# Expert weights in longer rows, into pairs of neighbouring buffers

## The chip, the cores and the metric

One core of a Trainium2 chip runs the whole program. The time is the device time of one execution in microseconds (us). Three executions of the kernel before are the measure it is held against.

## What is computed

Two transformer blocks run one after the other on 512 tokens of width 1024, batch 1, all in float32. The first has an attention with three branches and a linear recurrence (RG-LRU); the second has a chunked mLSTM, a differential attention and, at its end, a mixture of 32 experts, which is what the change is about:

```python
def hierarchical_moe(h, w_rg, b_rg, w_re, b_re, w_gate, w_up, w_down):
    hf = h.reshape(-1, d_)
    ...
    y = jnp.zeros_like(hf)
    for e in range(N_EXPERTS):                      # 32 experts, two of them per token
        act = jax.nn.silu(hf @ w_gate[e]) * (hf @ w_up[e])     # 1024 -> 256 each
        y = y + combine[:, e:e + 1] * (act @ w_down[e])        # 256 -> 1024
    return y.reshape(b_, s_, d_)
...
x = x + gate2 * hierarchical_moe(h2, ...)
```

Gate and up weights of one expert are 1024 x 512 floats (2 MB), its down weights 256 x 1024 (1 MB), so that the experts together are 100.7 MB of weights, each read once.

## The kernel before, in words

**Recording and planning.** The code doesn't issue instructions as it runs. Class `Plan` records every operation as a node with what it reads and writes (`record`, line 216), and `order` then places the nodes one after the other: at each step it takes, over the five engines, the node that can start first by its own prices, and gives its output tiles a buffer. `issue` (line 400) emits them all in that order; line 409 is therefore the line of every instruction in the profile, and groups go by tile names. Two nodes share a buffer by names like `t4.7`: a tile with that tag waits for all users of the tile before it.

**Buffers.** `SIZES` gives the tags: `t4` has 38 buffers of 128 x 1024 floats (4 KB in each of 128 partitions), `a2` 15 and `p2` 9 buffers of 128 x 512. Nearly everything large lives in `t4`: a loaded weight slab (`gt`, `gr`, `wp`), its two parts `h` and `l` in float32r (`slab`: high part by a cast, low part by a subtraction, so that three matmuls give float32 accuracy), the transposed hidden state `hTh`/`hTl` (`new_hT`), rows of `x`, and the expert tiles `wg`. Loads named in `FREE` (`wg`, `wd`) may be issued up to 9000 nodes early, as soon as a buffer is free.

**The experts** (`experts`, line 1804). The router places the tokens of two experts, i and i+16, in 128 rows, 64 each; there are 16 such rounds. A round gathers its rows from `x2d` in HBM (`fetch`: an indirect DMA of POOL into one of two tiles X), transposes them on PE into XT, multiplies them by the two experts' gate/up weights into H, activates, transposes (`aT`), multiplies by the down weights into two banks, scales into Y, and adds Y's rows to the output by an indirect DMA of POOL. In H the two experts use the two halves of PE's columns at once. Weights come by SP, and by SP alone:

```python
for q in range(4):                       # wg: 128 x 2 x 512, 4 KB rows, 512 KB a load
    for e in range(2):
        nc.sync.dma_start(ws[e], I["wgu"][i + 16 * e, q])
...
for k in range(2):                       # wd: 128 x 512, 2 KB rows, 256 KB a load
    for h in range(2):
        for e in range(2):
            nc.sync.dma_start(w, I["wd"][i + 16 * e, k][:, h * 512:(h + 1) * 512])
```

So a round has eight `wg` loads and eight `wd` loads. Completion of SP's loads is counted by eight semaphores in turn (DMAHW0 to DMAHW7); a load waits until the load eight before it has landed. `experts` runs once straight through; a loop behind it repeats it if an expert has more than 64 tokens, which doesn't occur here.

**What lies ahead of the first round.** `route_chunk` writes four pieces of normalised rows to `x2d` and the residual to the output, by SP's queue; `route`, `slots` and `weights` compute the row numbers `si` and the factors `wt` on DVE and PE. The first gather needs the four `x2d` writes and `si`.

Of the kernel before, what the change touches and what calls it, by code (L numbers as in the profile page):

```python
# [134 lines left out]
class Tile:  # L135
    def __init__(self, plan, tag, shape, dt, name, keep, given=None):
        self.plan, self.tag, self.name, self.dt, self.shape, self.keep = plan, tag, name, dt, list(shape), keep
        self.got = given
# [31 lines left out]

class Node:
# [7 lines left out]
class Plan:  # L179
# [20 lines left out]
    def tile(self, tag, shape, dt, name, keep=False):  # L200
        return Tile(self, tag, shape, dt, name, keep).view()
# [62 lines left out]
    def order(self):  # L264
# [9 lines left out]
        for nd in nodes:  # L274
            for t in nd.tiles:
# [5 lines left out]
                prof[t.tag][start:end] += 1  # L281
# [3 lines left out]
        for nd in nodes:  # L285
            for t in nd.births:
                rest[t.tag] += not nd.load
# [13 lines left out]
        while len(out) < N:  # L301
# [3 lines left out]
            for e, lst in ready.items():  # L305
# [4 lines left out]
                for nd in lst:  # L310
# [7 lines left out]
                    if nd.births:  # L318
                        ok = nd.load or nd.i - p < 400
                        need = {}  # L320
                        for t in nd.births:
# [3 lines left out]
                            k = need[t.tag] = need.get(t.tag, 0) + 1  # L325
# [7 lines left out]
                            s = max(s, tg.free[k - 1][0])  # L333
# [17 lines left out]
            for t in nd.births:  # L351
# [6 lines left out]
                t.slot = tg.free.pop(0)[1]  # L358
                rest[t.tag] -= not nd.load
                if p < t.first:  # L360
                    prof[t.tag][p:t.first] += 1
# [16 lines left out]
            for t in nd.tiles:  # L378
                t.left -= 1
                if t.left == 0 and not t.keep and self.tags[t.tag].space != "dram":  # L380
                    r = max(k.done[1] + (200.0 if k.done[2] == "PE" or t.space == "psum" else 130.0)
                            for k in [nd] + [k for _, k in t.writes + t.reads])
                    insort(self.tags[t.tag].free, (r, t.slot))
                    if p <= t.last:
                        prof[t.tag][p:t.last + 1] -= 1
# [122 lines left out]
class Net:  # L508
    def __init__(self, tc, ctx, I, out, upto="all", dbg=None):
# [5 lines left out]
        self.kept, self.stand = [], {}  # L515
# [9 lines left out]
    SIZES = {"t4": 38, "a2": 15, "p2": 9, "vm": 4, "sq128": 3, "c1k": 4}  # L525

    def start(self):

        self.nc = Plan(self.tc, self.scratch, self.stand)
        self.nc.tag("dram", "dram", [], self.make)  # L530
# [7 lines left out]
    def make(self, t):  # L538
        if t.space == "dram":
            return self.pools["dram"].tile(t.shape, t.dt, name=t.name)  # L540
        return self.pools[t.space].tile(t.shape, t.dt, name=t.name, tag=f"{t.tag}.{t.slot}", bufs=1)

    def tile(self, tag, shape, dt, name, keep=False, bufs=None, space="sbuf"):
        if tag not in self.nc.tags:
            self.bufs.setdefault(tag, bufs or self.SIZES[tag])
            kept = {t.slot for t in self.kept if t.tag == tag}
            self.nc.tag(tag, space, [k for k in range(self.bufs[tag]) if k not in kept], self.make)
        v = self.nc.tile(tag, shape, dt, name, keep)
# [4 lines left out]
    def t4(self, name, shape=(128, 1024), dt=F32, keep=False):  # L553
        return self.tile("t4", list(shape), dt, name, keep)

# [21 lines left out]
    def pair4(self, name):  # L577

        t = [self.t4(f"{name}{i}", (128, 2, 512), F32R) for i in range(2)]
        return [t[k // 2][:, k % 2, :] for k in range(4)]  # L580
# [1434 lines left out]
```

## Time and profile before

| | us |
|---|---|
| median of three executions | 1121.15 (1118.64 to 1123.18) |
| the profiled execution | 1121.38 |
| its span, first to last instruction | 1119.5 |
| PE busy | 1043.2 (93%) |
| DVE busy | 636.0 (57%) |
| ACT busy | 394.1 (35%) |
| POOL busy | 187.8 (17%) |
| HBM read | 212.91 MB, 206 GB/s over the span |

A span is the time in which instructions run; 1.9 us of the execution's time lie around it. Busy shares are means over the whole span, and stages differ: a table by stage tells more than the page. In a stage, the engine or queue that is never idle sets the pace; what others wait for there is the thing to look up. DMA share is the mean busy share of the core's 16 DMA engines, from the times of their packets, and can come out a little over 1.

### The profile page before, as it was taken

The page shows a single profiled execution, that of the slowest core. Times are in us where ns is not written, and L with a number is a line of the kernel's source. Part 1 is how long each engine was busy: PE and PEld are TensorE (multiplying, and loading weights), DVE is VectorE, ACT ScalarE, POOL GpSimd, SP SyncE. Part 2 cuts the span into 40 slices and gives each one's busy share as a digit, 9 for nine tenths or more (in the row PEclk, how much of TensorE's full clock was granted, in tenths as well). Part 3 has the DMA queues.
Part 4 walks back from the last instruction along what each step waited for, and adds up shares of the span by engine and source line. Part 5 has one row for each costly group of instructions (what it writes and reads, how often), then busy time and mean ns, then how long its engine had stood idle before and what let it go on. Part 6 is the DMA issues. An engine that isn't in the chain of part 4 may idle for free. (4 is left out here: it accounts for less than half of the span.)

```text
span 1119.5 us, 14485 instructions
## 1 busy us (share of the span) xinstructions
PE 1043.2 (93%) x5194; PEld 724.3 (65%) x5194; DVE 636.0 (57%) x1433; ACT 394.1 (35%) x803; POOL 187.8 (17%) x173
## 2 busy tenths in 40 slices
PE   9999999999999999999999999999996999877875
PEld 7776666777887777786687887788785333322221
DVE  4757788695654746976978876535714223222221
ACT  6235566562222326436653333222412112111110
POOL 1201134001011224401311001100201122210101
PEclk9998998999999999999999999999996999999997
DMA  9981100234444807160232423546699999999995
GB/s 350 339 323 43 39 1 20 76 99 132 122 139 162 274 38 280 53 263 11 94 147 85 164 95 113 169 131 225 227 359 366 323 368 343 365 376 346 387 368 166
DMA packets 77374, 223.43 MB, mean 200 GB/s; under 512 B 12164, under 2 KB 13772, under 8 KB 77296
## 3 DMA queue, kind: packets, MB, share of 16 engines
q1 hardware_dynamic: 72544, 213.94, 53.0%
q0 software_dynamic: 4608, 8.40, 3.1%
q8 instruction: 43, 0.70, 0.3%
q14 instruction: 35, 0.29, 0.1%
q10 hardware_dynamic: 144, 0.10, 0.0%
HBM read 212.91 MB, written 17.32 MB: 206 GB/s over the span
## 5 line engine op out<-in xcount | busy, mean ns | idle before, releaser
L409 PE MATMUL H<-wg,XT 128*64 128x512 f32 x512 | 128.8, 606 | 11.0 <-DMA wg<-in_wgu 8.0
L409 PE MATMUL b<-hTh,gth 128*128 128x512 f32 x464 | 122.9, 402 | 0.0
L409 PE MATMUL b<-hTl,gth 128*128 128x512 f32 x464 | 121.4, 398 | 0.0
L409 PE MATMUL b<-hTh,gtl 128*128 128x512 f32 x464 | 119.7, 397 | 0.0
L409 POOL TENSOR_TENSOR gtl<-gt,gth 128x1024 fp32r<-128x1024 f32 x23 | 57.5, 2501 | 262.6 <-ACT gth L409 243.5
L409 PEld LDWEIGHTS b<-hTh,gth 128*128 128x128 f32 x464 | 86.2, 189 | 23.7 <-issue 4.2
L409 PEld LDWEIGHTS b<-hTh,gtl 128*128 128x128 f32 x464 | 86.6, 188 | 20.4 <-issue 0.5
L409 PEld LDWEIGHTS b<-hTl,gth 128*128 128x128 f32 x464 | 86.2, 188 | 20.1 <-issue 0.9
L409 PEld LDWEIGHTS H<-wg,XT 128*64 128x64 f32 x512 | 37.7, 137 | 86.5 <-issue 52.4
L409 DVE TENSOR_SCALAR XT<-b,mod,mod 128x128 f32<-128x128 f32 x64 | 24.2, 408 | 78.4 <-PE H L409 69.0
L409 PE MATMUL b<-wd,aT 128*64 128x512 f32 x256 | 60.7, 612 | 7.7 <-ACT aT L409 5.0
L409 DVE SCALAR_TENSOR_TENSOR ada_acc<-ada_w,cols,ada_acc 128x1024 f32<-128x1024 f32 x42 | 60.2, 1434 | 8.5 <-DMA ada_w<-in_w_ada 8.5
L409 DVE SCALAR_TENSOR_TENSOR Y<-b,wt,gate 128x512 f32<-128x512 f32 x32 | 24.0, 751 | 68.1 <-PE b L409 65.0
L409 ACT ACTIVATE XT<-b,mod,mod 128x128 f32<-128x128 f32 x64 | 27.4, 459 | 88.5 <-PE H L409 71.1
L409 ACT ACTIVATE gth<-gt 128x1024 fp32r<-128x1024 f32 x53 | 55.4, 1050 | 6.7 <-DMA gt<-in_wb 6.7
L409 PE MATMUL b<-grh,hTh 128*128 128x512 f32 x192 | 56.1, 404 | 0.0
L409 PE MATMUL b<-grl,hTh 128*128 128x512 f32 x192 | 55.6, 399 | 0.0
L409 PE MATMUL b<-grh,hTl 128*128 128x512 f32 x192 | 55.0, 398 | 0.0
L409 POOL DMA_INDIRECT out_rows<-Y,si x16 | 25.3, 1583 | 159.3 <-DVE Y L409 144.0
L409 ACT ACTIVATE grh<-gr 128x1024 fp32r<-128x1024 f32 (+2 forms) x39 | 39.7, 1032 | 29.8 <-DMA gr<-in_wo 8.7
L409 DVE TENSOR_TENSOR gtl<-gt,gth 128x1024 fp32r<-128x1024 f32 x35 | 42.6, 1223 | 10.8 <-ACT gth L409 8.9
L409 DVE SCALAR_TENSOR_TENSOR mg<-mg,b 128x512 f32<-128x512 f32 x32 | 21.9, 686 | 43.4 <-PE b L409 43.4
(374 smaller groups left out, 1830.6 us busy)
## 6 DMA issues: line engine op xcount, KB each, us to landing
wg<-in_wgu SPq DMA_DIRECT2D x128, 512.0 KB
wd<-in_wd SPq DMA_DIRECT2D x128, 256.0 KB
gt<-in_wb SPq DMA_DIRECT2D x58, 512.0 KB
ada_w<-in_w_ada SPq DMA_DIRECT2D x48, 512.0 KB
gr<-in_wa SPq DMA_DIRECT2D x23, 512.0 KB
wp<-in_wp SPq DMA_DIRECT2D x16, 512.0 KB
gr<-in_wo SPq DMA_DIRECT2D x16, 512.0 KB
cw<-in_cmp_w SPq DMA_DIRECT2D x8, 512.0 KB
```

The source lines that it names most:

```text
L409: i = getattr(getattr(self.nc, eng), meth)(*[val(a) for a in args], **{k: val(v) for k, v in kw.items()})
```

## The change

Expert weights are laid out in HBM so that a `wg` load takes 1 MB in rows of 8 KB (four k-tiles of 512 columns) and a `wd` load 512 KB in rows of 4 KB (both halves h at once). Loads per round go from 16 to 8. For that a tile may be two neighbouring buffers wide: buffers are made as pairs (one allocation for buffers 2n and 2n+1), `a2` and `p2` become 16 and 8, and `wd` tiles alternate between them (every third in `p2`).

In the whole program, tiles that live together become one tile of two buffers (`t8`): high and low part of a slab, two row tiles of `load_rows`, quarters of `hT`, the two gather tiles X, and XT with Y. Single tiles take a half: `pick` gives out a half only where the other half is free or holds a tile of the same kind (`kind` says whether the type is float32r), and prefers a half whose neighbour is in use. `take` and `drop` keep count of a pair; while any half is in use the pair stays one allocation with one name, which is why many tiles in the changed program's order bear a neighbour's name (the names `gate2_4011` or `ada_w_5856` stand there for many tiles). Computation and its instructions on PE are the same.

```diff
+    def fits(self, k, kind):
+        return k >> 1 not in self.live or self.live[k >> 1][0] == kind
...
+    def pick(self, width, taken, kind):
+        if width == 1:
+            best = None
+            for r, k in self.free:
+                if k not in taken and self.fits(k, kind) and k ^ 1 not in taken:
+                    half = k >> 1 in self.live
+                    if best is None or r == 0.0 and half > best[2]:
+                        best = r, [k], half
+                    if r > 0.0 or half:
+                        break
+            return best and best[:2]
+        seen = set()
+        for r, k in self.free:
+            if k in taken:
+                continue
+            if k ^ 1 in seen:
+                return r, [k & ~1, k | 1]
+            seen.add(k)
+        return None
...
-                                    or len(tg.free) < k
+                                    or got is None
...
-            s = max(s, tg.free[k - 1][0])
+            s = max(s, got[0])
...
-    SIZES = {"t4": 38, "a2": 15, "p2": 9, "vm": 4, "sq128": 3, "c1k": 4}
+    UNITS = {"t4": 1024, "a2": 512, "p2": 512}
+    SIZES = {"t4": 38, "a2": 16, "p2": 8, "vm": 4, "sq128": 3, "c1k": 4}
...
+        pair, half = divmod(t.slot, 2)
+        if t.gen not in self.pairs:
+            self.pairs[t.gen] = self.pools[t.space].tile([128, 2 * u], F32, name=t.name, tag=f"{t.tag}.{pair}", bufs=1)
+        a = self.pairs[t.gen][:t.shape[0], half * u:half * u + t.row]
...
-        w, hi, lo = self.t4(name), self.t4(name + "h", dt=F32R), self.t4(name + "l", dt=F32R)
+        w, hl = self.t4(name), self.t8(name + "hl", (128, 2, 1024), F32R)
+        hi, lo = hl[:, 0], hl[:, 1]
...
-        x = [self.t4(f"{name}{c}") for c in range(NCH)]
+        x = [self.t8(f"{name}{c}", (128, 2, 1024)) for c in range(0, NCH, 2)]
...
-            for q in range(4):
+            for q in range(2):
                 ws = []
                 for e in range(2):
-                    ws.append(self.t4("wg", (128, 2, 512)))
+                    ws.append(self.t8("wg", (128, 4, 512)))
                     nc.sync.dma_start(ws[e], I["wgu"][i + 16 * e, q])
-                for k in range(2):
-                    kt = 2 * q + k
+                for k in range(4):
+                    kt = 4 * q + k
...
-                for h in range(2):
-                    for e in range(2):
-                        w = wd[k, h, e] = self.p2("wd") if k + h + e > 1 and k else self.a2("wd")
-                        nc.sync.dma_start(w, I["wd"][i + 16 * e, k][:, h * 512:(h + 1) * 512])
+                for e in range(2):
+                    w = self.tile("p2" if (4 * i + 2 * k + e) % 3 == 2 else "a2", [128, 2, 512], F32, "wd", width=2)
+                    nc.sync.dma_start(w, I["wd"][i + 16 * e, k])
+                    for h in range(2):
+                        wd[k, h, e] = w[:, h]
...
-        self.X = [self.t4(f"X{k}", keep=True) for k in range(2)]
-        self.XT, self.Y = self.t4("XT", keep=True), self.t4("Y", keep=True)
+        X, Z = [self.t8(n, (128, 2, 1024), keep=True) for n in ("X", "XTY")]
+        self.X = [X[:, k] for k in range(2)]
+        self.XT, self.Y = Z[:, 0], Z[:, 1]
```

How the order of instructions moves is shown at three places.

SP, just ahead of the first round, before, behind the last write of `x2d` and three `wd` loads: the last row is the 35th `wg` load of the program.

```order
L409 DMA wg_7542<-in_wgu 128x1024 [waits DMAHW6_49]
L409 DMA wg_7544<-in_wgu 128x1024 [waits DMAHW7_49]
L409 DMA wg_7549<-in_wgu 128x1024 [waits DMAHW0_49]
L409 DMA wg_7551<-in_wgu 128x1024 [waits DMAHW1_49,DVE_49,PE_49]
L409 DMA wg_7556<-in_wgu 128x1024 [waits DMAHW2_49]
L409 DMA wg_7558<-in_wgu 128x1024 [waits DMAHW3_49]
L409 DMA wg_7560<-in_wgu 128x1024 [waits DMAHW4_49]
L409 DMA wg_7591<-in_wgu 128x1024 [waits DMAHW5_49,PE_49]
```

The same place in the changed kernel, from the last write of `x2d` on; the first `wg` row that waits for PE is the 17th of the program.

```order
L458 DMA x2d_6788<-x2n_6934 128x1024 [waits DMAHW2_49,Activation_49]
L458 DMA wd_6968<-in_wd 128x1024 [waits DMAHW3_49,PE_49]
L458 DMA wd_6986<-in_wd 128x1024 [waits DMAHW4_49]
L458 DMA wg_7018<-in_wgu 128x2048 [waits DMAHW7_49,DMAHW5_49]
L458 DMA wg_7020<-in_wgu 128x2048 [waits DMAHW6_49,DMAHW0_49]
L458 DMA wg_7061<-in_wgu 128x2048 [waits PE_49]
L458 DMA wg_7063<-in_wgu 128x2048
L458 DMA wg_7076<-in_wgu 128x2048 [waits DMAHW1_49,PE_49]
```

Before, 34 loads of 512 KB stand ahead of the first that waits for PE's expert work; now 16 loads of 1 MB do. Two loads now wait for the writes out of the buffers they take (DMAHW7, DMAHW0).

SP in a late round, before: eight `wd` loads and then eight `wg` loads, each waiting for the load eight before it.

```order
L409 DMA wd_8471<-in_wd 128x512 [waits DMAHW3_49,PE_49]
L409 DMA wd_8476<-in_wd 128x512 [waits DMAHW4_49,PE_49]
L409 DMA wd_8484<-in_wd 128x512 [waits DMAHW5_49,PE_49]
L409 DMA wd_8487<-in_wd 128x512 [waits DMAHW6_49]
L409 DMA wd_8494<-in_wd 128x512 [waits DMAHW7_49,PE_49]
L409 DMA wd_8502<-in_wd 128x512 [waits DMAHW0_49,PE_49]
L409 DMA wd_8509<-in_wd 128x512 [waits DMAHW1_49,PE_49]
L409 DMA wd_8512<-in_wd 128x512 [waits DMAHW2_49,PE_49]
L409 DMA wg_8516<-in_wgu 128x1024 [waits DMAHW3_49]
L409 DMA wg_8531<-in_wgu 128x1024 [waits DMAHW4_49]
```

The same in the changed kernel.

```order
L458 DMA wg_7909<-in_wgu 128x2048 [waits DMAHW5_49]
L458 DMA wg_7911<-in_wgu 128x2048 [waits DMAHW6_49]
L458 DMA wd_7913<-in_wd 128x1024 [waits DMAHW7_49,PE_49]
L458 DMA wd_7915<-in_wd 128x1024 [waits DMAHW0_49,PE_49]
L458 DMA wd_7917<-in_wd 128x1024 [waits DMAHW1_49,PE_49]
L458 DMA wd_7919<-in_wd 128x1024 [waits DMAHW2_49,PE_49]
L458 DMA wg_7935<-in_wgu 128x2048 [waits DMAHW3_49]
L458 DMA wg_7946<-in_wgu 128x2048 [waits DMAHW4_49]
```

Four and four loads alternate, so that any eight in a row hold four of each size.

PE, from the down matmuls of the last round but one to the first H matmul of the last, before (`b<-wd,aT` is the down product, `H<-wg,XT` the gate/up product):

```order
L409 MATMUL b_8869<-wd_8810,aT_8867 64x512 [waits DMAHW3_49,Activation_49]
L409 MATMUL b_8869<-wd_8815,aT_8867 64x512 [waits DMAHW4_49]
L409 MATMUL b_8876<-wd_8823,aT_8867 64x512 [waits DMAHW5_49,PE_49]
L409 MATMUL b_8876<-wd_8826,aT_8867 64x512 [waits DMAHW6_49]
L409 MATMUL b_8869<-wd_8833,aT_8867 64x512 [waits DMAHW7_49]
L409 MATMUL b_8869<-wd_8836,aT_8867 64x512 [waits DMAHW0_49]
L409 MATMUL b_8876<-wd_8843,aT_8867 64x512 [waits DMAHW1_49]
L409 MATMUL b_8876<-wd_8846,aT_8867 64x512 [waits DMAHW2_49]
L409 MATMUL H_8898<-wg_8850,XT_7570 64x512 [waits DMAHW3_49,PE_49]
L409 MATMUL H_8898<-wg_8860,XT_7570 64x512 [waits DMAHW4_49]
```

The same in the changed kernel (XT lies in the pair named XTY).

```order
L458 MATMUL H_8151<-wg_7986,XTY_7036 64x512 [waits DMAHW7_49]
L458 MATMUL H_8151<-wg_8043,XTY_7036 64x512 [waits DMAHW4_49]
L458 MATMUL b_8157<-wd_7992,aT_8154 64x512 [waits DMAHW0_49,Activation_49]
L458 MATMUL b_8157<-wd_7997,aT_8154 64x512 [waits DMAHW1_49]
L458 MATMUL b_8157<-wd_8005,aT_8154 64x512 [waits DMAHW2_49]
L458 MATMUL b_8157<-wd_8029,aT_8154 64x512 [waits DMAHW3_49]
L458 MATMUL b_8162<-wd_7992,aT_8154 64x512 [waits PE_49]
L458 MATMUL b_8162<-wd_7997,aT_8154 64x512
L458 MATMUL b_8162<-wd_8005,aT_8154 64x512
L458 MATMUL b_8162<-wd_8029,aT_8154 64x512
L458 MATMUL H_8151<-wg_7986,XTY_7036 64x512
L458 MATMUL H_8151<-wg_8043,XTY_7036 64x512
```

The first k-tile of the last round now stands ahead of the down product of the round before it.

## Rows read from the trace of the kernel before

**Rows 1.** The page: busy time (us) and share of the span.
```profile
PE 1043.2 (93%) x5194; PEld 724.3 (65%) x5194; DVE 636.0 (57%) x1433; ACT 394.1 (35%) x803; POOL 187.8 (17%) x173
```

**Rows 2.** By stage: length, PE, PEld, DVE, ACT, POOL busy, PE clock, DMA share, GB/s.
```profile
112.00:400.00 288.00, 277.81 (x1443) 214.42 (x1442) 202.33 (x415) 125.85 (x239) 50.81 (x32) 0.99 0.32 104
...
780.00:840.00 60.00, 60.00 (x300) 49.15 (x298) 27.55 (x33) 18.51 (x29) 10.45 (x12) 1.00 0.77 295
...
900.00:960.00 60.00, 59.30 (x293) 22.07 (x293) 19.16 (x43) 12.37 (x31) 14.20 (x12) 1.00 1.00 361
...
1020.00:1080.00 60.00, 48.27 (x187) 14.95 (x188) 13.72 (x28) 9.67 (x22) 6.22 (x4) 1.00 1.03 380
```

**Rows 3.** POOL in order of time: start us, us, operation [idle before, releaser].
```profile
882.78 1.63 POOL L409 DMA_INDIRECT out_rows<-Y,si  x1 [5.91 <-DVE Y L409]
...
944.16 1.59 POOL L409 DMA_INDIRECT out_rows<-Y,si  x1 [6.79 <-DVE Y L409]
...
1038.65 1.55 POOL L409 DMA_INDIRECT out_rows<-Y,si  x1 [13.61 <-DVE Y L409]
...
1109.30 1.56 POOL L409 DMA_INDIRECT out_rows<-Y,si  x1 [14.47 <-DVEq L1891]
```

**Rows 4.** SP, POOL and PE in order of time at the start of the experts.
```profile
848.12 0.32 SPq L409 DMA_DIRECT2D x2d<-x2n  x1
...
857.80 1.29 POOL L409 DMA_INDIRECT X<-x2d,si  x1 [10.88 <-DMA wd<-in_wd]
...
866.87 7.72 PE L409 MATMUL H<-wg,XT 128*64 128x512 f32 x32
...
869.46 0.85 SPq L409 DMA_DIRECT2D wg<-in_wgu  x2
```

**Rows 5.** SP's waits, 860 to 870 us: total us, times, longest.
```profile
SPq L409 <- PE H L409: 10.2, 2, 9.8
```

**Rows 6.** PE in order of time, the last down product.
```profile
1102.65 5.35 PE L409 MATMUL b<-wd,aT 128*64 128x512 f32 x16 [0.54 <-ACT aT L409]
```

**Rows 7.** DMA, stretches 1052:1060 and 1064:1066; loads issued in 866:1102.
```profile
DMA packets 915, 3.27 MB, mean 408 GB/s; under 512 B 102, under 2 KB 102, under 8 KB 915
...
DMA packets 433, 0.79 MB, mean 394 GB/s; under 512 B 49, under 2 KB 49, under 8 KB 433
...
wg<-in_wgu SPq DMA_DIRECT2D x94, 512.0 KB
wd<-in_wd SPq DMA_DIRECT2D x104, 256.0 KB
```

**Rows 8.** SP in order of time, a late round.
```profile
1053.43 10.96 SPq L409 DMA_DIRECT2D wd<-in_wd  x8
1065.27 4.97 SPq L409 DMA_DIRECT2D wg<-in_wgu  x8
```

**Rows 9.** By stretch, columns as in rows 2: five short stretches.
```profile
889.00:893.00 4.00, 4.00 (x22) 1.52 (x22) 1.18 (x3) 0.40 (x2) 0.17 (x1) 1.00 0.65 208
895.00:900.00 5.00, 5.00 (x29) 2.16 (x26) 0.45 (x2) 0.64 (x2) 1.57 (x1) 1.00 0.88 271
927.00:936.00 9.00, 9.00 (x46) 3.02 (x42) 1.56 (x3) 1.76 (x4) 1.59 (x1) 1.00 0.81 289
1012.00:1016.00 4.00, 2.35 (x10) 0.89 (x10) 1.25 (x4) 0.39 (x1) 0.00 (x0) 1.00 0.58 170
1066.00:1068.00 2.00, 0.41 (x2) 0.20 (x2) 1.25 (x3) 0.49 (x2) 0.00 (x0) 1.00 1.00 290
```

**Rows 10.** DMA queues, 862 to 866 us: packets, MB, share of 16 engines.
```profile
q1 hardware_dynamic: 311, 1.14, 71.3%
q0 software_dynamic: 270, 0.48, 31.6%
```

**Rows 11.** PE's waits, 200 to 840 us: total us, times, longest.
```profile
PE b L409 <- DVE hm L409: 1.9, 1, 1.9
```

**Rows 12.** SP's waits, 889 to 893 us: total us, times, longest.
```profile
SPq L409 <- PE b L409: 4.6, 1, 4.6
```

More of the change, by code (lines that the diff above doesn't have):

```diff
@@ L135, with __init__ @@
 class Tile:
-    def __init__(self, plan, tag, shape, dt, name, keep, given=None):
+    def __init__(self, plan, tag, shape, dt, name, keep, given=None, width=1):
         self.plan, self.tag, self.name, self.dt, self.shape, self.keep = plan, tag, name, dt, list(shape), keep
-        self.got = given
+        self.got, self.width, self.kind = given, width, dt == F32R
         self.space = plan.tags[tag].space
@@ L168, in __init__, with take, drop @@
         self.free = [(0.0, k) for k in slots]
+        self.live = {}
+    def fits(self, k, kind):
+        return k >> 1 not in self.live or self.live[k >> 1][0] == kind
+    def take(self, slots, kind, count):
+        v = self.live.setdefault(slots[0] >> 1, [kind, 0, None])
+        v[1] += len(slots)
+        if v[2] is None:
+            v[2] = next(count)
+        return v[2]
+    def drop(self, slots):
+        v = self.live[slots[0] >> 1]
+        v[1] -= len(slots)
+        if v[1] == 0:
+            del self.live[slots[0] >> 1]
+    def pick(self, width, taken, kind):
[17 more added lines that the diff above has]
+        return None
 class Node:
@@ L280, in order @@
                 start = 0 if t.placed else t.first
-                prof[t.tag][start:end] += 1
+                prof[t.tag][start:end] += t.width
         for nm, p in prof.items():
@@ L286, in order @@
             for t in nd.births:
-                rest[t.tag] += not nd.load
+                rest[t.tag] += 0 if nd.load else t.width
         ready = {e: [] for e in ("PE", "ACT", "DVE", "POOL", "SP")}
@@ L357, in order @@
                     continue
-                t.slot = tg.free.pop(0)[1]
-                rest[t.tag] -= not nd.load
+                slots = tg.pick(t.width, (), t.kind)[1]
+                t.gen = tg.take(slots, t.kind, self.count)
+                t.slot = slots[0]
+                tg.free = [x for x in tg.free if x[1] not in slots]
+                rest[t.tag] -= 0 if nd.load else t.width
                 if p < t.first:
-                    prof[t.tag][p:t.first] += 1
+                    prof[t.tag][p:t.first] += t.width
             if e == "ACT" and alt[2] == "activation":
@@ L382, in order @@
                             for k in [nd] + [k for _, k in t.writes + t.reads])
-                    insort(self.tags[t.tag].free, (r, t.slot))
+                    self.tags[t.tag].drop([t.slot + k for k in range(t.width)])
+                    for k in range(t.width):
+                        insort(self.tags[t.tag].free, (r, t.slot + k))
                     if p <= t.last:
-                        prof[t.tag][p:t.last + 1] -= 1
+                        prof[t.tag][p:t.last + 1] -= t.width
             out.append(((s, len(out)), nd, alt))
@@ L514, in __init__ @@
         self.scratch = bacc.Bacc("TRN2", target_bir_lowering=False, num_devices=1)
-        self.kept, self.stand = [], {}
+        self.kept, self.stand, self.pairs, self.count = [], {}, {}, itertools.count()
         self.bufs = {}
@@ L554, in t4, with t8 @@
         return self.tile("t4", list(shape), dt, name, keep)
+    def t8(self, name, shape, dt=F32, keep=False):
+        return self.tile("t4", list(shape), dt, name, keep, width=2)
     def a2(self, name, dt=F32, keep=False):
@@ L577, in pair4 @@
     def pair4(self, name):
-        t = [self.t4(f"{name}{i}", (128, 2, 512), F32R) for i in range(2)]
-        return [t[k // 2][:, k % 2, :] for k in range(4)]
+        t = self.t8(name, (128, 4, 512), F32R)
+        return [t[:, k, :] for k in range(4)]
     def bank(self, name="b"):
@@ L672, in load_rows @@
     def load_rows(self, src, name):
-        x = [self.t4(f"{name}{c}") for c in range(NCH)]
+        x = [self.t8(f"{name}{c}", (128, 2, 1024)) for c in range(0, NCH, 2)]
+        x = [x[c // 2][:, c % 2] for c in range(NCH)]
         for c in range(NCH):
@@ L689, in new_hT @@
     def new_hT(self, src=None):
[L691 to L692 removed]
+        self.h2 = [[self.t8(f"hT{n}{i}", (128, 4, 512), F32R) for i in range(2)] for n in "hl"]
+        self.h_hi, self.h_lo = [[t[k // 4][:, k % 4, :] for k in range(KT)] for t in self.h2]
         self.wn = self.c1k("wn", [128, KT, 32])
@@ L786, in hT_chunk @@
             for j in range(2):
-                hi, lo = [t[2 * half + j][:, :, cs] for t in self.h2]
+                hi, lo = [t[half][:, 2 * j:2 * j + 2, cs] for t in self.h2]
                 nc.scalar.activation(hi, h[:, 2 * j:2 * j + 2], AF.Copy)
```

36 lines of the change are left out of this document (25 added, 11 removed).

## Prediction

> **What bounds the kernel now.** I read the busy shares of the page first [rows 1]: PE is busy for 93% of the span. The table by stage [rows 2] shows that this is an average of two limits. From 112 to 400 us PE works 277.81 of 288 us and the DMA share is 0.32; from 780 to 840 us PE works all of 60 us. From 900 to 960 us both are full (PE 59.30 of 60, DMA 1.00). From 1020 to 1080 us PE has dropped to 48.27 of 60 us while the DMA share is 1.03. So PE sets the time up to about 955 us, and the stream of expert weights sets it from there to the end.
>
> The pace of the 16 expert rounds says the same. Each ends with a scatter [rows 3]: 882.78 to 944.16 us is five rounds of 12.3 us, 1038.65 to 1109.30 us four rounds of 17.7 us. A round needs 8 x 512 KB of up/gate rows and 8 x 256 KB of down rows, 6.29 MB; at 12.3 us that would be 511 GB/s, more than any stretch moves. The early rounds live on a stock of loaded tiles, the late ones wait for the stream. When the stock is full, and when the first buffer comes free, is seen at the start of the experts [rows 4]: the last x2d write is issued at 848.12, the gather at 857.80, and PE begins H at 866.87. SP issues its next load at 869.46; before it, from 860 on, it waits for PE's H, 10.2 us in two waits [rows 5]. All up/gate buffers are full then. So the end is: the first free buffer (869.46), plus the time to stream what isn't yet loaded, plus the tail behind the last transfer. The last Y is multiplied from 1102.65 [rows 6] and the last scatter goes out at 1109.30 [rows 3]. The chain of waits shows only that scatter and is of no help.
>
> My sum is made against the profiled execution, 1121.38 us (span 1119.5), which is 0.02% from the median 1121.15.
>
> **Longer rows.** A stretch that moves only 4 KB rows (813 packets besides 102 small ones) runs at 408 GB/s, one that moves 2 KB rows at 394 GB/s [rows 7]. That is 2.451 and 2.538 us per MB: doubling 2 KB saves 0.087 us per MB. A fixed cost per packet gives half of that, 0.043, for 4 to 8 KB. Nothing in the trace moves 8 KB weight rows, so this is an estimate, between nothing and the same 0.087. In 866 to 1102 us 94 up/gate loads (49.3 MB) and 104 down loads (27.3 MB) are issued [rows 7]. Saved: 27.3 x 0.087 + 49.3 x 0.043 = **4.5 us** (2.4 to 6.7). The Trainium skill's page "DMA: Bandwidth & Descriptors", section "Specifications", gives 512 B as the least transfer for line rate; by that this term would be nothing. The 394 against 408 GB/s speaks against it, by little.
>
> **Bytes in flight.** In the order SP's load waits for the semaphore of the load eight before (DMAHW0 to 7 in turn). With eight 256 KB tiles out, 2.1 MB or 5 us of work is queued. SP's eight down loads take from 1053.43 to 1064.4, and the next up/gate load starts at 1065.27 [rows 8]; from 1066 to 1068 the rate is 290 GB/s [rows 9], that is 0.6 us lost against 408. Where it is worse the engines run dry: shares of 0.65, 0.88, 0.81 and 0.58 in four stretches of 4, 5, 9 and 4 us [rows 9] leave 1.4 + 0.6 + 1.7 + 1.7 = 5.4 us of all engines' time unused. Seven more changes from down to up/gate loads lie outside these four, and I count them at 0.5 us each: 3.5 us. With the change eight loads in flight are always four of 1 MB and four of 512 KB. I leave 0.9 us of the 8.9 and take **-8.0 us** (from -2.5 to -8.9).
>
> **Fewer buffers for the stock.** t4 has 38 buffers. Before, X0, X1, XT and gate5 take four and Y its own only later: 34 up/gate tiles, 17 MB binary, are loaded ahead; the 35th waits for PE. In the changed kernel 19 pairs lose one to X, one to XT/Y and one whose half holds gate5: 16 pairs, and the 17th load waits for PE. So 1.05 MB more has to come after the start: at 408 GB/s **+2.6 us**. The down tiles keep 6 MB binary (24 tiles, 12 pairs).
>
> **The start.** A pair comes free after four k-tiles and not two. Eight k-tiles of the first H take 7.72 us [rows 4], so two more take **+1.9 us**. Counted in the order up to the last x2d write, the loads carry 14 MB binary and not 13, and 1 MB of down rows and not 0.75: together, in decimal, 1.3 MB x 2.451 = 3.2 us, less 14.7 MB x 0.043 = 0.6. Some of the loads stand earlier in the order, where DMA time is idle (share 0.77 from 780 to 840 us, [rows 2]), so I take half of the 2.6: 1.3 us later, and the gather with it. While both gathers move (862 to 866), 270 packets of the gathers' queue pass beside 311 of the loads [rows 10], eight per gather and engine; if each lets an 8 KB packet by in place of a 4 KB one (4 KB on one of 16 engines at 408 GB/s is 0.16 us) that is 1.3 us, of which I take half, since the loads are about to stop. Together **+2.0 us** (0 to +5). The Trainium skill's same page, section "Queues, rings and completion order", says that an engine goes round its queue rows packet by packet; the trace agrees (311 to 270).
>
> **The tail.** The down loads are last in both. In the changed order PE multiplies the last but one round's Y behind the first up/gate pair of the last round, and the last H needs four k-tiles after its last 1 MB lands: 4 x 0.9 us (7.72 us for eight, [rows 4]) in place of two. H is then ready 2 us later against the last down tile, which has little slack now. **+1.5 us** (0 to +3).
>
> **The first 840 us.** Work on PE is the same; in the recorded order 11 casts of whole tiles go from ACT to DVE and POOL has six operations fewer. Between 200 and 840 us PE waits for no weight: its longest single wait is 1.9 us, for hm from DVE [rows 11]. So loads that come a little later are hidden, at **0 us** (-4 to +6: two waits fewer of that size, or three more).
>
> **Sum:** -4.5 - 8.0 + 2.6 + 1.9 + 2.0 + 1.5 = -4.5, so 1121.4 - 4.5 = 1116.9 us; I say 1117. A difference of 0.5% (5.6 us) is about what a measurement of this kernel can tell from no change, and the forecast lies just inside.
>
> **Rivals.**
> First, the dry spells come from buffers and from the scatters, not from the depth. For it: SP waits 4.6 us for PE between 889 and 893 [rows 12], and no depth cures a full stock. Then only 2 to 3 us of that term come: 1121.4 - 4.5 - 2.5 + 8.0 = 1122.4, no change.
> Second, larger gain: 8 KB rows save the full 0.087 us per MB (-2.2), the x2d write and the gather are no later, because the four up/gate loads that now stand ahead of gate5's fill idle DMA time (-2.0), and the tail is hidden (-1.5): 1116.9 - 5.7 = 1111.2.
> Third, longer rows move no faster, since the engines run at a rate of their own already; the rest of the sum stands: 1116.9 + 4.5 = 1121.4, no change. The step from 2 to 4 KB rows [rows 7] speaks against it. This is what the 512 B rule of the Trainium skill's page "DMA: Bandwidth & Descriptors" would give.
> Fourth, slower: in the first 840 us a half whose neighbour is still in use, or of the other kind (F32R beside F32), can't be given out, loads are issued later, and PE waits for weights in its dense stages. One such wait I price at 1.9 us, the longest there now [rows 11]; from six on (11.4 us) the gain of 4.5 and the 5.6 above it are spent: 1128.3. At eight it is 1116.9 + 15.2 = 1132.1. Against it: there is no wait for a weight from 200 to 840 us now, so the loads have room.
>
> **How the numbers follow.** The forecast, 1117 with a spread of 1112 to 1121: 0.44, of which 0.22 falls under 1115.5 and 0.22 within 0.5%. First rival 0.12 (no change), second 0.22 (faster), third 0.04 (no change), fourth 0.18 (0.16 slower, 0.02 still within). That gives faster 0.44, same 0.40 and slower 0.16. The range takes in the first three and the light end of the fourth, and reaches below the second for the unknown first part: 1106 to 1128, with about 1 in 10 on either side.
>
> **What would show it.** Longer rows: over 410 GB/s in pure up/gate stretches. Depth: no stretch of DMA share under 0.9 after 880 us besides the scatters. Stock: SP silent from before 858 until 1 or 2 us after H's first four k-tiles, with the engines dry for 6 to 8 us around 870. Start: H at 868 to 870, if the first part ends where it does now. Tail: Y 2 us behind the last load. The forecast is wrong if H starts well off 869 (then the first part moved), or if the late rounds stay at 17 to 18 us.

## The result, and the profile after

The changed kernel takes **1160.25 us** (1155.67 to 1161.88, six executions) against 1122.16 for the kernel before beside it: a ratio of 1.0323 [1.0295, 1.0351]: 38 us between the medians, 33 to 39 by the interval. The forecast was 1117 us, with a range up to 1128. The profiled execution took 1156.96 us, its span is 1155.0, 35.5 us longer than before.

The page answers to [rows 1]: PE works 3 us more, and idles 33 us more.

```profile
PE 1046.2 (91%) x5194; PEld 727.7 (63%) x5194; DVE 642.8 (56%) x1451; ACT 382.3 (33%) x791; POOL 191.9 (17%) x167
```

By stage, columns as in [rows 2], with a stretch at the end that had no counterpart:

```profile
112.00:400.00 288.00, 274.10 (x1403) 208.78 (x1400) 204.36 (x416) 119.04 (x231) 45.15 (x23) 0.96 0.29 98
...
900.00:960.00 60.00, 59.14 (x286) 21.31 (x287) 13.89 (x34) 10.68 (x29) 9.00 (x8) 1.00 1.02 403
1020.00:1080.00 60.00, 44.89 (x190) 14.62 (x188) 12.69 (x28) 8.06 (x19) 6.87 (x5) 0.86 1.01 390
1110.00:1150.00 40.00, 13.12 (x54) 3.83 (x50) 6.39 (x10) 0.77 (x2) 6.24 (x4) 0.67 0.25 37
```

The loads did get faster: 403 and 390 GB/s where 361 and 380 stood. But from 112 to 400 us PE idles 13.9 us in place of 10.2, and from 1110 to 1150 us PE is busy for 13 of 40 us and the DMA share is 0.25, while the program isn't over. Where that comes from is read off four landmarks. The rows give count, duration and first and last start; of before first, H alone (its x2d writes and scatters are in [rows 4] and [rows 3]):

```profile
L409 PE MATMUL H<-wg,XT x512: 592/592/1116, 866.9 to 1099.6; 128*64 128x512 f32 x171
```

```profile
L458 SPq DMA_DIRECT2D x2d<-x2n x3: 320/320/429, 861.5 to 866.4; - x3
...
L458 PE MATMUL H<-wg,XTY x512: 592/592/1117, 889.1 to 1116.7; 128*64 128x512 f32 x171
...
L458 POOL DMA_INDIRECT out_rows<-XTY,si x16: 1552/1576/1637, 905.6 to 1144.5; - x16
```

| stretch, us | before | after | difference |
|---|---|---|---|
| start to the last x2d write | 848.1 | 866.4 | +18.3 |
| x2d write to the first H | 18.8 | 22.7 | +3.9 |
| first H to the last H | 232.7 | 227.6 | -5.1 |
| last H to the last scatter | 9.7 | 27.8 | +18.1 |
| last scatter to the end | 10.2 | 10.5 | +0.3 |

So two losses of 18 us each, at places where I had put 0 and +1.5.

**The tail** is seen on VectorE (DVE), in order of time:

```profile
1117.79 0.88 DVE L458 SCALAR_TENSOR_TENSOR act<-act,H 128x256 f32<-128x256 f32 x2 [10.45 <-ACT act L458]
1118.58 1.40 DVE L458 SCALAR_TENSOR_TENSOR XTY<-b,wt,gr 128x512 f32<-128x512 f32 x2
1127.13 1.41 DVE L458 SCALAR_TENSOR_TENSOR XTY<-b,wt,gr 128x512 f32<-128x512 f32 x2 [7.14 <-DMA out_rows<-XTY,si]
1135.07 1.41 DVE L458 SCALAR_TENSOR_TENSOR XTY<-b,wt,gr 128x512 f32<-128x512 f32 x2 [6.53 <-DMA out_rows<-XTY,si]
1142.59 1.41 DVE L458 SCALAR_TENSOR_TENSOR XTY<-b,wt,gr 128x512 f32<-128x512 f32 x2 [6.11 <-DMA out_rows<-XTY,si]
```

Four rounds' Y are written after the last round's act, though PE had three of these products ready earlier. There is one Y, so each write waits until the scatter of the one before has landed, some 8 us apiece. Over all rounds DVE waits 49.8 us for scatters (2.7 before):

```profile
  DMA out_rows<-XTY,si: 49.8, 7
```

The order says the same. DVE's rows from the last rounds of the changed kernel; behind the last one shown stand five more Y rows and nothing else of the experts:

```
1286 L458 SCALAR_TENSOR_TENSOR act_8013<-act_8013,H_7954 128x256 x2
1287 L458 SCALAR_TENSOR_TENSOR act_8061<-act_8061,H_8010 128x256 x2
...
1290 L458 SCALAR_TENSOR_TENSOR XTY_7036<-b_7975,wt_7014,gr_6487 128x512
1291 L458 SCALAR_TENSOR_TENSOR XTY_7036<-b_7983,wt_7014,gr_6487 128x512
...
1296 L458 SCALAR_TENSOR_TENSOR act_8181<-act_8181,H_8151 128x256 x2
1297 L458 SCALAR_TENSOR_TENSOR XTY_7036<-b_8038,wt_7014,gr_6487 128x512
1298 L458 SCALAR_TENSOR_TENSOR XTY_7036<-b_8045,wt_7014,gr_6487 128x512
1299 L458 SCALAR_TENSOR_TENSOR XTY_7036<-b_8098,wt_7014,gr_6487 128x512
```

**The first part.** PE's busy time up to the last x2d write, before and after (columns as in [rows 2]):

```profile
0.00:848.10 848.10, 826.34 (x4234) 644.85 (x4234) 568.49 (x1264) 354.81 (x707) 145.91 (x141) 0.99 0.44 154
```

```profile
0.00:866.40 866.40, 833.79 (x4236) 648.47 (x4237) 578.26 (x1282) 344.91 (x696) 149.94 (x135) 0.99 0.42 150
```

Of the 18.3 us, 10.8 are idle time (32.6 for 21.8) and 7.5 are longer work. Most of it arises early, in the attention block that ends with the last write of PT, before first:

```profile
86.10:192.20 106.10, 99.36 (x732) 72.15 (x732) 86.49 (x321) 66.51 (x194) 26.29 (x25) 0.94 0.09 26
```

```profile
87.50:204.90 117.40, 105.66 (x749) 75.14 (x749) 95.57 (x334) 65.36 (x192) 23.56 (x16) 0.93 0.07 23
```

That is 11.3 us of the 18.3, 5.0 of them idle and 6.3 longer work. The clock may be part of the longer work; no run prices it by itself. In two stretches of after the granted clock is 0.51 and 0.69 of 2.4 GHz, all or part of the time at the lower level of 1.2 GHz:

```profile
110.00:120.00 10.00, 8.57 (x74) 6.35 (x72) 7.23 (x31) 5.60 (x19) 3.27 (x4) 1.00 0.01 2
120.00:130.00 10.00, 9.16 (x33) 4.85 (x33) 6.46 (x29) 3.59 (x12) 1.22 (x2) 0.51 0.30 79
155.00:165.00 10.00, 9.64 (x52) 6.13 (x51) 7.13 (x24) 5.70 (x17) 5.63 (x3) 0.69 0.15 52
```

Before, the same kind of fall stands at 85 to 95 and 175 to 185 us, both at 0.66. PE's longest waits up to 866 us, and a shorter one further down the list, are

```profile
PE b L458 <- DVE P L458: 3.9, 4, 1.4
PE b L458 <- POOL P L458: 3.6, 3, 1.3
PE b L458 <- DVE qk L458: 3.4, 1, 3.4
PE b L458 <- ACT mh L458: 3.2, 1, 3.2
...
PE b L458 <- ACT grhl L458: 1.8, 1, 1.8
```

No wait is for a load itself; they are for results of other engines. One of them goes back to a weight: `grhl` holds the two parts of a weight slab, and ACT made them late because it had waited for the load:

```profile
446.86 1.06 ACT L458 ACTIVATE grhl<-gr 128x1024 fp32r<-128x1024 f32 x1 [2.64 <-DMA gr<-in_wa]
```

It cost PE 1.8 us; the kernel before has no wait of this kind.

### The profile page after: what moved, and what is told of

Same layout as the page of the kernel before. It is cut to its first block, busy times and chain, and to the rows that moved or that the text cites. A ratio compares the mean times of both kernels' runs of the same rounds, so it can differ in the third digit from the quotient of the medians.

```text
span 1155.0 us, 14246 instructions
## 1 busy us (share of the span) xinstructions
PE 1046.2 (91%) x5194; PEld 727.7 (63%) x5194; DVE 642.8 (56%) x1451; ACT 382.3 (33%) x791; POOL 191.9 (17%) x167
## 5 line engine op out<-in xcount | busy, mean ns | idle before, releaser
L458 PE MATMUL b<-hTh,gthl 128*128 128x512 f32 x928 | 238.9, 400 | 0.2 <-DVE PT L458 0.2
L458 PEld LDWEIGHTS b<-hTh,gthl 128*128 128x128 f32 x928 | 173.3, 189 | 44.0 <-issue 4.4
L458 PE MATMUL H<-wg,XTY 128*64 128x512 f32 x512 | 121.8, 614 | 8.5 <-DVE XTY L458 7.6
L458 PE MATMUL b<-hTl,gthl 128*128 128x512 f32 x464 | 121.0, 398 | 0.0
L458 PE MATMUL b<-grhl,hTh 128*128 128x512 f32 x368 | 99.3, 402 | 1.8 <-ACT grhl L458 1.8
L458 PEld LDWEIGHTS b<-hTl,gthl 128*128 128x128 f32 x464 | 86.2, 188 | 20.1 <-issue 1.1
L458 PEld LDWEIGHTS b<-grhl,hTh 128*128 128x128 f32 x368 | 67.1, 188 | 18.1 <-ACT grhl L458 2.2
L458 PE MATMUL b<-wd,aT 128*64 128x512 f32 x256 | 65.3, 655 | 10.2 <-DVE XTY L458 8.6
L458 PE MATMUL b<-grhl,mh 128*128 128x512 f32 x256 | 70.8, 406 | 3.2 <-ACT mh L458 3.2
L458 DVE TENSOR_SCALAR XTY<-b,mod,mod 128x128 f32<-128x128 f32 x64 | 23.6, 406 | 67.2 <-PE H L458 53.2
L458 PEld LDWEIGHTS b<-grhl,mh 128*128 128x128 f32 x256 | 48.3, 193 | 14.3 <-ACT mh L458 3.6
L458 DVE SCALAR_TENSOR_TENSOR XTY<-b,wt,gr 128x512 f32<-128x512 f32 x32 | 22.7, 745 | 57.2 <-DMA out_rows<-XTY,si 49.8
L458 PE MATMUL b<-grhl,hTl 128*128 128x512 f32 x184 | 51.4, 398 | 0.0
```

Of the source, the lines that this page charges most:

```text
L458: i = getattr(getattr(self.nc, eng), meth)(*[val(a) for a in args], **{k: val(v) for k, v in kw.items()})
```

## Experiments

Medians of the kernel before beside the runs were 1123.5 to 1123.9 us.

**1. A scatter's landing time in the planner.** `order` books every DMA on one bus, behind all loads already booked; with loads twice as large the booked landing of a scatter goes further back, and with it the next Y. First try:

```diff
-                bus = max(bus, s + dur + (650.0 if e == "SP" else 4800.0)) + byts / 360.0
-                end = bus + 910.0
+                if e == "SP":
+                    bus = max(bus, s + dur + 650.0) + byts / 360.0
+                    end = bus + 910.0
+                else:
+                    bus += byts / 360.0
+                    end = s + dur + 7000.0
```

> The changed kernel, but the planner takes a scatter or gather of POOL to land 7 us after its issue, and no longer books it behind every weight load that is queued on its one bus. Only the written order of the expert rounds can change by this; tiles, loads and their sizes stay. In the changed kernel the last four Y writes of VectorE run out one after the other behind the last H (scatters at 1120.59, 1129.01, 1136.94, 1144.46 us, PE's last H at 1117). Theory A (order): the planner books a scatter behind up to eight loads, which now hold twice the bytes, so it puts VectorE's Y writes behind the act and XT of later rounds, and they bunch at the end. Then here every Y stands next to its own round's act, VectorE waits under 10 us in all for scatters (49.8 now), the last scatter is issued 9 to 12 us after the last H (before: 9.7, now 27.8), and the median falls by 15 to 20 us, to 1140-1145. Rival B (queue): a scatter really lands late, because its rows wait behind 8 KB packets; then the order is no matter, the landing stays at 9 to 10 us, the waits move to the next round and the median stays within 5 us of 1160. Both expect the last x2d write where it is, at 863-870 us.

Measured: 1154.56 us. The tail is A's: last H 1139.5, last scatter 1147.5, 8.0 us; DVE waits 6.4 us for scatters. The median is off, because x2d came at 883.3: the branch also held for early loads that other engines issue. Put right, with `if alt[2] == "indirect_dma_start"` for the new branch, so that it holds for gathers and scatters alone:

> As the run with the 7 us landing, but put right: there the new estimate held for every DMA that isn't SyncE's, so the loads that other engines issue at the start were planned anew as well, and the first part moved (last x2d write 883.3 us against 866.4). Here it holds for gathers and scatters alone, so the first part's order is the changed kernel's: x2d at 863-870. Theory A (order): VectorE waits under 10 us for scatters, the last scatter comes 8 to 10 us after the last H, and H's first to last lasts about 228 us as in the changed kernel: median 1140-1145. Rival B2 (the stream pays for the better order): H's first to last lasts 233 us as in the first try, and the median is 1146-1150.

Measured: **1142.88 us** (1142.20 to 1146.44), x2d at 866.6.

```profile
L462 PE MATMUL H<-wg,XTY x512: 592/592/1116, 890.6 to 1122.2; 128*64 128x512 f32 x171
...
L462 POOL DMA_INDIRECT out_rows<-XTY,si x16: 1552/1586/1627, 906.6 to 1130.4; - x16
...
  DMA out_rows<-XTY,si: 9.6, 3
...
DMA to landing us min/median/max: 6.0/9.5/10.8
```

The last scatter comes 8.2 us after the last H. A scatter still takes 9.5 us to land, so the landing was not the cause; the order was. From first H to last scatter it is 239.8 us (255.4 in the changed kernel): the order of the Ys cost 15.6 us. First to last H is 231.6, not the 228 that A expected and nearer to B2's 233: H was quicker in the changed kernel, probably because Y work had been put behind it. The median is A's.

**2. Half-size loads into the same pairs.**

```diff
-                    nc.sync.dma_start(ws[e], I["wgu"][i + 16 * e, q])
+                    for g in range(2):
+                        nc.sync.dma_start(ws[e][:, 2 * g:2 * g + 2], I["wgu"][i + 16 * e, q][:, 1024 * g:1024 * g + 1024])
...
-                    nc.sync.dma_start(w, I["wd"][i + 16 * e, k])
...
+                        nc.sync.dma_start(w[:, h], I["wd"][i + 16 * e, k][:, 512 * h:512 * h + 512])
```

> The changed kernel with the same pairs, but each pair is filled by two loads again (up/gate 512 KB in rows of 4 KB, down 256 KB in rows of 2 KB), so eight loads in flight hold half the bytes. The first part is as in the changed kernel (x2d at 863-870 us). Theory A (order, by the bytes that the planner books ahead of a scatter): the booking halves, so the Ys stand where they stood before, the tail falls from 27.8 to 9-12 us behind the last H (-17), while the rate from 900 to 960 us falls from 400-406 to about 387 GB/s and costs 5 to 10 us: median 1148-1154. Rival E (XT and Y in one tile make VectorE wait for the scatter): the pairs are as they were, so the waits for scatters stay near 50 us and the median at 1160-1170.

Measured: 1151.24 us; no wait for a scatter at all, the last one 8.0 us after the last H, 373 GB/s from 900 to 960 us. That is A, and E falls: XT and Y share a pair here too. (x2d came at 873.5, beyond the 863 to 870 that was expected, and the rate is lower than the 387 expected.)

**3. The first part: pairs or counts?** Singles again in `slab`, `load_rows`, `pair4` and `new_hT`, as in the kernel before; and, in the kernel before, the new counts alone:

```diff
-        w, hl = self.t4(name), self.t8(name + "hl", (128, 2, 1024), F32R)
-        hi, lo = hl[:, 0], hl[:, 1]
+        w, hi, lo = self.t4(name), self.t4(name + "h", dt=F32R), self.t4(name + "l", dt=F32R)
```

> The changed kernel, but the first part takes its tiles singly again: slabs' high and low parts, the rows of x, the pairs of a four-tile and the transposed h come from single 4 KB buffers; only the experts' weights, X and XT/Y are pairs. The buffers' counts (16 of a2, 8 of p2) stay. Theory C (pairs cost the first part 18 us): the last x2d write moves from 866.4 back to 848-853 us and the median to 1140-1148. Rival D (the ninth p2 buffer): the tiles of the block that is slow now, P and PT, lie in p2, which lost one of its nine buffers; then nothing comes back, x2d stays at 862-870 and the median at 1155-1165.

Measured: 1201.74 us, x2d at 902.4. Both theories fail: it got 36 us worse. PE's idle time up to there is 61.3 us, and from 824 to 844 us it is busy for 9.17 of 20 us; why wasn't followed further, so this run says only that breaking pairs up under the new rules is no way back.

```diff
-    SIZES = {"t4": 38, "a2": 15, "p2": 9, "vm": 4, "sq128": 3, "c1k": 4}
+    SIZES = {"t4": 38, "a2": 16, "p2": 8, "vm": 4, "sq128": 3, "c1k": 4}
```

> The kernel before with one number pair altered: 16 buffers of a2 and 8 of p2 (15 and 9 before), nothing else. The block from 86 to 192 us scales P on VectorE and POOL out of p2 tiles; in the changed kernel it lasts 117.4 us, before 106.1. Rival D (the ninth p2 buffer): that block lasts 112 to 118 us here, the last x2d write is at 855-866 us (848.1 before), and the median rises to 1129-1140. Theory C (pairs): nothing moves, x2d at 846-850, median within 4 us of 1122.

Measured: 1131.18 us, ratio 1.0062 [1.0042, 1.0082]; x2d at 853.9, the block up to the last PT 111.0 us. The median is D's, block and x2d fall about a microsecond short of it, and 5.8 us of the 18 are there. Only 0.6 of the 5.8 are idle time of PE (22.4 for 21.8); the rest is longer work, at a granted clock of 0.91 in the block where 0.94 stood. `a2` changed in the same edit, so the 5.8 belong to the two counts together. The same count from the other side, on top of the scatters' own time:

```diff
-    SIZES = {"t4": 38, "a2": 16, "p2": 8, "vm": 4, "sq128": 3, "c1k": 4}
+    SIZES = {"t4": 38, "a2": 14, "p2": 10, "vm": 4, "sq128": 3, "c1k": 4}
```

> As the run with the scatters' own time, and with 10 buffers of p2 and 14 of a2 (8 and 16 in the changed kernel; 9 and 15 before). Theory D (the attention block lacks p2 buffers): the block up to the last PT ends at 192 to 198 us (204.9 in the changed kernel, 192.2 before), x2d comes 6 to 8 us earlier than in the run beside it, and the median is lower by as much, 1132-1138. Theory F (what the first part loses comes from halves of pairs that hold each other up, not from the count): x2d moves by less than 3 us.

Measured: 1135.45 us, 7.4 us less, as D said; last PT 193.8, x2d 858.3, 8.3 us earlier. Ten us remained.

**4. The other half's release.** A pair is one allocation; a new tile in it waits for the users of both halves. `pick` reckons with the half it hands out:

```diff
-            for r, k in self.free:
+            when = {k: r for r, k in self.free}
+            for r, k in sorted((max(r, when.get(k ^ 1, 0.0)), k) for r, k in self.free):
```

> The changed kernel, but where the planner opens a pair for a single tile it takes the later of the two halves' release times for both. A pair is one allocation, so the chip waits for both halves; the changed planner reckons with the half it hands out alone. Theory F (the plan overlooks these waits, and they cost the first part several us on the chip): x2d comes 6 us or more earlier, at 852-860 us, and the median falls to 1146-1154. Theory D (such waits hardly occur; the count of p2 and the order do it): x2d stays within 4 us of 866 and the median within 4 us of 1160. The tail is left as it is (27 to 28 us from the last H to the last scatter).

Measured: **1133.24 us**, x2d at 837.7, 28.7 us earlier and more than F asked for; the tail is 27.6 us. PE's work up to there:

```profile
0.00:837.70 837.70, 822.91 (x4237) 642.89 (x4238) 574.84 (x1270) 347.05 (x701) 142.69 (x142) 1.00 0.44 155
```

Idle time is 14.8 us, less than half of 32.6: 17.8 of the 28.7 us are idle time and 10.9 are shorter work. To see how much a mere change of order does, two runs price each VectorE operation 1 ns dearer, in the kernel before and in the changed one:

```diff
-        return 70 + n * (0.52 if fast else 1.042) + (58 * ones if meth != "tensor_tensor_reduce" else 0)
+        return 71 + n * (0.52 if fast else 1.042) + (58 * ones if meth != "tensor_tensor_reduce" else 0)
```

> The kernel before, with each VectorE operation priced 1 ns dearer in the planner (71 in place of 70 ns ahead of the elements): nothing in the program is meant to change but the order, by chance. It tells how far the first part moves by the order alone. Theory G (the first part's 18 us are largely the luck of another order): x2d moves by 5 us or more, in either direction, and the median by as much. Theory C or D (the loss has a cause in pairs or buffer counts): x2d at 846-851 us, median within 3 us of 1123.

> The changed kernel with each VectorE operation priced 1 ns dearer in the planner: another order, by chance, with no repair. Theory F (hidden waits): they stay whatever the order, x2d at 858 us or later, median 1150-1168. Theory G (the luck of one order): x2d falls to 850 or earlier in this other order, and the median to 1145 or less.

Measured: 1122.64 us with x2d at 846.7; and 1155.85 us with x2d at 863.0 and 32.9 us of idle time. The order by itself moved x2d by 1.4 and 3.4 us. Two orders of the changed kernel thus lie 15 to 20 us behind two of the kernel before, so the loss is hardly one unlucky order; the last run of experiment 5 shows an order that moves x2d by more.

The repair alters two things, the pair picked and the time booked. With the pick alone, behind the sorting above:

```diff
-                        best = r, [k], half
+                        best = when[k], [k], half
```

> The changed kernel, with one half of the halves' repair: where the planner opens a pair for a single tile it picks the pair whose later half is released first, but its timetable still reckons with the release of the half it hands out. Theory F1 (the choice of pair removes the waits on the chip): last x2d write at 836-846 us as with the whole repair (837.7), PE's idle time up to it near 15 us (32.6 in the changed kernel), median 1130-1140. Rival F2 (the timetable does it: whoever knows of the wait puts other work ahead of it): x2d at 858 us or later, idle time near 30 us, median 1150-1162. The tail is as in the changed kernel.

Measured: 1151.87 us, x2d 861.3, idle 28.8. It is F2: the pick alone takes 3.8 us of the idle time away, and the booked time is needed for the rest. That a planner which knows of the wait puts other work ahead of it is the likely reason; no row shows it.

**5. Both repairs**, the scatters' own time (the second form) and the other half's release: alone, then with the half loads of 2, with the counts of 3, and with the dearer VectorE operation of 4.

> The two repairs together: the planner waits for both halves of a pair that it opens, and it books gathers and scatters by a landing time of their own. Theory F with A (hidden waits for the other half, and Y writes put off): last x2d write at 836-840 us as with the halves alone, from there to the span's end 273.7 us as with the scatters alone (866.6 to 1140.3), so a span near 1111 us and a median of 1110 to 1116, below the kernel before (1123). Theory G (the earlier x2d was the luck of one order): x2d moves again by 8 us or more and the median lies at 1120 or above.

Measured: **1116.42 us** (12 executions), ratio to the kernel before 0.9951 [0.9926, 0.9975]; x2d at 839.5, last scatter 7.9 us behind the last H: F with A, the median just above the 1110 to 1116 expected. Beside it:

> The two repairs, with each pair filled by two loads (rows of 4 KB and 2 KB, half the bytes in flight): against the run with the repairs alone, only the loads differ. By my prediction's terms (4.5 us for longer rows, 8.0 for bytes in flight) it is 12 us slower: H's first to last 243 us in place of 232, median 1122-1128. Rival H (the larger loads bring less in a good order): H's first to last 235 to 237 us, median 3 to 6 us above the run beside it.

Measured: 1123.68 us, 7.3 more, between the two. By stage, whole loads first, then half loads:

```profile
900.00:960.00 60.00, 57.43 (x286) 21.75 (x282) 18.29 (x43) 10.98 (x27) 15.14 (x12) 1.00 1.02 394
960.00:1020.00 60.00, 46.59 (x216) 15.83 (x218) 14.53 (x29) 9.23 (x22) 9.44 (x7) 1.00 1.02 390
1020.00:1080.00 60.00, 44.77 (x178) 14.92 (x174) 14.44 (x30) 9.19 (x22) 4.66 (x3) 0.97 1.01 382
```

```profile
900.00:960.00 60.00, 53.71 (x268) 21.52 (x266) 15.16 (x34) 10.79 (x26) 15.58 (x13) 0.97 0.99 350
960.00:1020.00 60.00, 46.16 (x210) 14.65 (x206) 15.71 (x35) 8.55 (x20) 6.95 (x6) 1.00 1.01 363
1020.00:1080.00 60.00, 45.17 (x185) 13.64 (x186) 13.24 (x27) 9.61 (x22) 6.21 (x4) 0.97 1.01 364
```

The DMA share is about 1 in both, so most of the gain is packets that got quicker. But a share can come out over 1, and a mean of 1.00 over 60 us hides short gaps. In stretches of 8 us the half loads have three gaps between 882 and 1082 us, where no such stretch of the whole loads is under 0.99:

```profile
922.00:930.00 8.00, 8.00 (x44) 3.18 (x40) 3.28 (x8) 2.35 (x6) 2.63 (x2) 1.00 0.90 264
946.00:954.00 8.00, 5.74 (x32) 2.77 (x32) 0.18 (x1) 1.83 (x4) 3.64 (x3) 1.00 0.87 274
1058.00:1066.00 8.00, 4.66 (x20) 1.44 (x20) 2.07 (x5) 0.77 (x2) 0.00 (x0) 1.00 0.88 310
```

They leave 0.8 + 1.0 + 1.0 = 2.8 us of all engines' time unused. The Trainium skill's page "DMA: Bandwidth & Descriptors", section "Specifications", gives 512 B as the least transfer for line rate. The measured 390 against 363 GB/s, rows of 8 and 4 KB against 4 and 2, speaks against a rate that is flat from there on. Rows and bytes in flight change together here, and no run parts them.

> The two repairs and 10 buffers of p2 with 14 of a2. Theory D (the attention block lacks p2 buffers): the last PT ends 3 us or more earlier than in the run with the repairs alone, and the median is 3 to 8 us lower. Theory F (once the halves are counted, 8 buffers do): within 3 us of that run.

Measured: 1120.50 us. The last PT came 6.3 us earlier, x2d 5.5 us later than beside it; neither theory. With both halves booked, more of `p2` brought nothing in this order; by how much another order moves x2d is seen next.

> The two repairs with each VectorE operation priced 1 ns dearer: another order, by chance. Theory F (the repair itself moves the first part): x2d at 835-846 us again, PE's idle time up to it 20 us or less, and the median at 1111-1121, below the kernel before. Theory G (that order was lucky): x2d at 850 us or later and a median at 1123 or above.

Measured: 1125.40 us, 1.0015 [0.9994, 1.0035]; x2d 850.2, idle 23.6. G, for the gain over the kernel before: the repaired kernel won it in one order and not in another (with 10 of `p2`, a third order, the ratio is 0.9966 [0.9948, 0.9983]). Here the order alone moved x2d by 10.7 us. Between the two orders with the dearer VectorE operation, without and with the repairs, x2d goes from 863.0 to 850.2 us, 12.8 us where the first order gave 26.9. Orders with both halves booked put x2d at 837.7, 839.5, 839.7, 845.0 and 850.2 us, all others of the changed kernel at 858.3 to 902.4. That the repair helps is shown; how much of the 18.3 us it makes up depends on the order, and that the pairs then beat the kernel before is not shown.

## Why the prediction was wrong

**"The first 840 us", 0 (-4 to +6): +18.3.** This step failed. I looked for loads that come late, found that PE waits for no weight, and called the rest hidden. The loss is in what other engines owe PE. The waits I read began at 200 us, and 11.3 of the 18.3 us arise before 205. Booking both halves' release took 27 to 29 us off in one order and 12.8 in another; the altered counts of `a2` and `p2` cost 5.8 us in the kernel before. I had seen that pairs are one allocation, and that `a2` and `p2` change; I used the first for the loads alone and the second not at all. The fourth rival had the place right (halves in the first 840 us) and the mechanism all but wrong: of its waits for weights one occurs, 1.8 us by way of `grhl`, where six were asked for. No single wait in the trace names the other half, since a wait is put down to the instruction that came last; what is shown is the idle time with and without the booking, 32.6 and 14.8 us.

**"The tail", +1.5 (0 to +3): +18.1.** This failed too. I read the order of PE and SP there and saw that the last Y product stands behind the next round's first k-tile. DVE's order, which I didn't read at that place, has four Ys in a row. The booking rule that made it stands in `order`, and the size of the loads is its input: with half loads in the same pairs no Y waits. With a scatter's own time the stretch from first H to last scatter fell by 15.6 us.

**"Longer rows" and "Bytes in flight", -12.5 together: -7.0.** That is the first H to the last scatter, 240.5 us with both repairs against 247.5 with half loads. Direction right, size too large. The pure up/gate rate is above 410 as I said:

```profile
898.00:903.00 5.00, 4.94 (x25) 1.76 (x25) 2.19 (x7) 1.89 (x5) 0.99 (x1) 1.00 1.00 424
```

From 896 to 1104 us no 8 us have a DMA share under 0.98, so the short dry spells of [rows 9] are gone. By the gaps in experiment 5, "Bytes in flight" was worth some 2.8 us and not 8.0, an estimate from one order; the rest of the 7.0 goes to quicker packets. The half loads keep the old depth and lose less than the 5.4 us of [rows 9]; that speaks for the first rival in part, and no run alters the depth alone.

**"Fewer buffers for the stock", +2.6, with the tail's +1.5: +5.1.** Half loads with both repairs take 247.5 us from first H to last scatter, the kernel before 242.4, with loads of the same size. What pairs cost the experts is somewhat more than I had put, if the planner's other prices for scatters, which the two runs don't share, count for little.

**"The start", +2.0: +3.9** from the last x2d write to the first H; with half loads and the repairs it is 19.4 us, that is +0.6, so it is the large loads around the gather. The +1.9 for the pair comes behind the first H: SP's next load follows it by 4.9 us where 2.6 stood [rows 4], +2.3.

```profile
894.02 0.81 SPq L458 DMA_DIRECT2D wg<-in_wgu  x2
```

The engines run dry as foreseen, but for longer:

```profile
884.00:896.00 12.00, 8.78 (x36) 3.79 (x38) 1.36 (x4) 1.50 (x4) 0.98 (x1) 0.68 0.31 91
```

At a share of 0.31, 8.3 us of all engines' time are lost there (6 to 8 foreseen): the stock is full when the first part ends, and any delay of the first part is idle time of the DMA engines.

So the terms for loads and buffers net -12.5 + 2.6 + 1.9 + 2.0 + 1.5 = -4.5; the mended kernel has -1.9 (242.4 to 240.5) and +3.7 at the start, +1.8, and 8.6 us from a first part whose order is as good as it is by luck. That its median of 1116.42 is close to the forecast of 1117 is chance. The three repaired orders with whole loads, at 0.9951, 0.9966 (10 of `p2`) and 1.0015 of the kernel before, lie between the forecast (0.996) and the no change of the first and third rivals, and don't decide between them.

## What to carry to other kernels

When a planner writes the order, a change of tile or load size is an input to its bookkeeping: ask for every resource that it books (bus, buffers, halves) what the new size makes it believe, and read the order of every engine at the end of the program, VectorE's too. Buffers that share an allocation are released together, and a timetable that doesn't know it loses more than it shows in any one wait. Before a gain of half a per cent is believed, alter a price by one nanosecond and measure another order.

## What the hardware showed

A scatter took longer to land beside larger loads: its median from issue to landing is 8.0 to 8.6 us in the five runs with loads of 512 and 256 KB, and 9.1 to 9.6 us in the eleven with 1 MB and 512 KB. The Trainium skill's page "DMA: Bandwidth & Descriptors", section "Queues, rings and completion order", has an engine go round its queues packet by packet. Larger packets would then cost the smaller queue time, and the two groups of medians agree with it; no run here changes the packets alone. In the changed kernel TensorE's granted clock was 0.51 from 120 to 130 us, the lower of its two levels, after a stretch of 10 us in which PE was busy for 8.57.
